# The gate blocks of layer 1, taken in pairs by seven block products over halves of features and tokens

## The chip, the cores and the metric

The kernel runs on one core of a Trainium2 chip. The metric is the device time of one execution in microseconds (us), here the median of several executions on the chip. The instructions of a core are spread over engines with a queue each: TensorE (PE, matrix products; its weight loads are shown as PEld), VectorE (DVE), ScalarE (ACT), GpSimd (POOL) and SyncE (SP, which issues most of the transfers). Each engine works through its own queue in order; engines wait for one another by semaphores.

## What is computed

The reference is one step of a two-layer encoder over 512 prompt and 64 sample tokens. The change lies in layer 1, whose input projection gives four things: the query latent `cq`, the key and value latent `ckv`, the rotary key `kr` and a `gate` of 2048 features.

```python
def odd_layer(x, past, w_in, q_norm_w, kv_norm_w, w_uq, w_ukv, w_out, ln_g, ln_b):
    cq, ckv, kr, gate = split_cols(x @ w_in, SPLIT1)      # 512, 512, 64, 2048 columns
    cq = rms_norm(cq, q_norm_w)
    ckv = rms_norm(ckv, kv_norm_w)
    q = (cq @ w_uq).reshape(b, t, C_HEADS, QK_NOPE + QK_ROPE)
    q_rope = rope(q[..., QK_NOPE:], q_pos)
    kr = rope(kr, q_pos)
    ...
    kv = (lat @ w_ukv).reshape(b, p_len + t, C_HEADS, QK_NOPE + V_DIM)
    ...
    o = o.reshape(b, t, C_WIDTH) * jax.nn.silu(gate)
    y = layer_norm(ALPHA * x + o @ w_out, ln_g, ln_b)
    return y, (ckv, kr)
```

All of it is fp32.

## The kernel before

The activations lie transposed in SBUF: 2048 features as 16 tiles of 128, by T = 576 tokens (512 prompt, 64 sample), in two halves of HALF = 288. TensorE has no fp32 product of full width, so each number is kept as a high part that TensorE takes (`xh`, `whi`) and a remainder (`xl`, `wlo`), and each product is three matmuls: high by high, high by remainder, remainder by high (`mm3`, L175 to L179). A matmul here takes a weight block of 128x128 and 288 tokens.

Weights come from memory in units of 128x1024, which is eight 128x128 blocks: SP loads the unit into a `wraw` tile (L96, two buffers), ScalarE rounds it into `whi` (L110), VectorE takes the remainder into `wlo` (L111). `whi` and `wlo` have four buffers each, so the ScalarE rounding of a unit waits until TensorE is done with the unit four places back. An output block of 128 features (`dense_block`, L153) takes two units, 16 feature tiles and two token halves: 96 matmuls into the two banks of one PSUM tile `pd` (`psd`, two buffers), and then a function (`post`) evacuates the tile.

Layer 1 begins with `quad` (L1085), which forms the four `cq` blocks beside the last layer norm of layer 0. Then, in this order: four blocks of `ckv` (L1244 ff., the last of them starts `c_norm`, which normalises the latent, splits it into `ar[8]` to `ar[15]` and stores it), one block for `kr` with its rotation (`post_kr`, `finish_kr`), and 16 gate blocks. `post_gate` (L1254 to L1258) takes a finished gate block through `silu_from` (L637 to L639: a scaled copy, a tanh and one VectorE operation) and SP stores it in `gts`. Then come the rotary queries in eight `half_unit` pieces (L1275 ff.), each with a copy out of PSUM (L1291), a swap of halves by transfers and a rotation on POOL and DVE (L1237 to L1239), and then the attention, head by head, which multiplies its output by the gate (L1344). Background work (`spawn`, `tick`) is woven in by generators, and a scheduler of the framework orders the instructions of each engine. Waits go by tile: whoever writes a tile waits for the last one that read any part of it.

## Time and profile before

| | |
|---|---|
| median of 3 runs | 2431.32 us (2430.07 to 2433.47) |
| the profiled execution | 2431.8 us |
| its span in the trace | 2430.0 us, so 1.8 us lie around it |
| PE busy | 2387.2 us, 98% of the span |
| DVE, ACT, POOL busy | 1213.7, 825.1, 438.9 us |

Busy times are sums over an engine's instructions. In the trace, consecutive matmuls overlap: one takes some 0.3 us from its start to its end, while the next starts 0.13 us after it. So the time of a run of matmuls is read from the spacing of their starts, and a wait of TensorE shows as a gap between starts. A window view gives, for a stretch of the execution, how long each engine was busy in it and at what share of its full clock TensorE was granted (PEclk). A row of a group of instructions says how long the engine had sat idle just before them, and what ended that. The lines of the profile are those of the kernel before.

### The profile page before, as it was taken

Reading aid. Unit: us, or ns where it says so; the run is one execution under the profiler, and the core shown is the slowest. Engines: PE = TensorE matmul, PEld = TensorE weight load, DVE = VectorE, ACT = ScalarE, POOL = GpSimd, SP = SyncE. Lnnn points to the kernel's source line nnn. Section 1 sums busy time; section 2 is a strip of 40 time slices with the busy share of each in tenths; the row PEclk is TensorE's granted clock in tenths of the full one; section 3 lists DMA queues with packets and bytes.
Section 4 is the critical chain, followed back from the end, with each engine's and each line's share of the span. In section 5 each row is a group of like instructions: output and inputs, shape, how many; then the busy total and the mean of one; then the engine's idle time right before and its main releaser. Section 6 shows DMA issues by size and latency. Waiting matters only on the chain. (4 is left out here: it accounts for less than half of the span.)

```text
span 2430.0 us, 43034 instructions
## 1 busy us (share of the span) xinstructions
PE 2387.2 (98%) x17978; PEld 2358.6 (97%) x17978; DVE 1213.7 (50%) x2290; ACT 825.1 (34%) x1462; POOL 438.9 (18%) x429
## 2 busy tenths in 40 slices
PE   9999999999999999999999999899999999999997
PEld 8999999999999999999999999899999999999996
DVE  6579784664845433434532223824224665654236
ACT  5442232332323333333431212332222454443233
POOL 0001161523515100000011223400001000001323
PEclk9999999999999999999999999999999999999998
DMA  6322242333323322322543332423334321122232
GB/s 211 113 81 79 92 139 83 124 106 104 133 76 128 110 100 91 100 91 91 170 146 97 103 102 81 152 80 127 103 108 136 121 69 60 63 72 79 103 121 79
DMA packets 96642, 256.69 MB, mean 106 GB/s; under 512 B 11520, under 2 KB 20768, under 8 KB 96448
## 3 DMA queue, kind: packets, MB, share of 16 engines
q1 hardware_dynamic: 94816, 251.44, 30.9%
q8 instruction: 141, 2.31, 0.4%
q10 hardware_dynamic: 1632, 2.51, 0.4%
q14 instruction: 53, 0.43, 0.1%
HBM read 216.37 MB, written 34.87 MB: 103 GB/s over the span
## 5 line engine op out<-in xcount | busy, mean ns | idle before, releaser
L179 PE MATMUL pd<-xh,whi 128*128 128x288 f32 x4128 | 894.7, 298 | 6.4 <-ACT whi L135 4.9
L179 PE MATMUL pd<-xh,wlo 128*128 128x288 f32 x4128 | 890.6, 296 | 0.0
L179 PE MATMUL pd<-xl,whi 128*128 128x288 f32 x4128 | 888.3, 296 | 0.0
L111 DVE TENSOR_TENSOR wlo<-wraw,whi 128x1024 fp32r<-128x1024 f32 x307 | 383.1, 1249 | 693.5 <-ACT whi L110 690.4
L179 PEld LDWEIGHTS pd<-xh,whi 128*128 128x128 f32 x4128 | 664.8, 188 | 12.3 <-ACT whi L135 5.2
L179 PEld LDWEIGHTS pd<-xh,wlo 128*128 128x128 f32 x4128 | 665.3, 188 | 1.0
L179 PEld LDWEIGHTS pd<-xl,whi 128*128 128x128 f32 x4128 | 664.5, 188 | 1.2 <-DVE xl L1347 0.2
L110 ACT CAST whi<-wraw 128x1024 fp32r<-128x1024 f32 x308 | 322.3, 1048 | 949.6 <-PE pd L179 922.0
L179 PE MATMUL pd<-ar,whi 128*128 128x288 f32 (+1 forms) x1120 | 211.1, 306 | 6.3 <-DVE xl L1367 4.3
L998 POOL TENSOR_TENSOR f<-f 128x576 f32<-128x576 f32 (+1 forms) x26 | 60.0, 2306 | 687.0 <-DVE f L991 687.0
L179 PEld LDWEIGHTS pd<-ar,whi 128*128 128x128 f32 x1120 | 170.3, 190 | 7.6 <-issue 3.9
L179 PE MATMUL pd<-ar,wlo 128*128 128x288 f32 (+1 forms) x560 | 125.6, 304 | 0.0
L179 PEld LDWEIGHTS pd<-ar,wlo 128*128 128x128 f32 x560 | 92.6, 189 | 0.0
L991 DVE SCALAR_TENSOR_TENSOR f<-f,pd 128x576 f32<-128x576 f32 (+3 forms) x35 | 23.3, 667 | 119.1 <-PE pd L179 91.2
L1406 PE MATMUL pd<-whi,ar 128*128 128x256 f32 (+1 forms) x384 | 74.1, 285 | 0.0
L625 DVE SCALAR_TENSOR_TENSOR f<-f,cw 128x579 f32<-128x579 f32 x72 | 61.4, 853 | 1.2
L1237 POOL TENSOR_TENSOR f<-f 128x576 f32<-128x576 f32 (+1 forms) x9 | 17.5, 1948 | 235.8 <-DMA f<-f 231.6
L1406 PEld LDWEIGHTS pd<-whi,ar 128*128 128x128 f32 (+1 forms) x384 | 57.9, 180 | 0.4
L1406 PE MATMUL pd<-wlo,ar 128*128 128x256 f32 (+1 forms) x192 | 54.3, 283 | 0.0
L739 DVE TENSOR_SCALAR G<-R,ncn 128x128 f32<-128x128 f32 (+1 forms) x160 | 46.9, 363 | 13.2 <-PE pt L758 6.9
L353 ACT ACTIVATE s<-ps,nmc 128x128 f32<-128x128 f32 (+4 forms) x80 | 40.7, 509 | 33.1 <-DVE nmc L1337 32.6
L331 ACT COPY pt<-pt 128x128 f32<-128x128 f32 (+1 forms) x64 | 27.4, 428 | 69.8 <-PE pt L330 64.1
(335 smaller groups left out, 2865.6 us busy)
## 6 DMA issues: line engine op xcount, KB each, us to landing
wraw<-in_wall SPq DMA_DIRECT2D x316, 512.0 KB, 3.5
f<-in_xT SPq DMA_DIRECT2D x32, 288.0 KB, 4.6
R<-rows SPq DMA_DIRECT2D x32, 288.0 KB, 3.3
mixs<-f SPq DMA_DIRECT2D x24, 288.0 KB, 3.2
f<-mixs SPq DMA_DIRECT2D x24, 288.0 KB, 5.9
ea<-rows SPq DMA_DIRECT2D x32, 144.0 KB, 3.2
ys<-f SPq DMA_DIRECT2D x16, 288.0 KB, 2.3
gts<-f SPq DMA_DIRECT2D x16, 288.0 KB, 3.9
```

The lines of the kernel that those rows point to most:

```text
L110: A.copy(hi[:, c], r)
L111: eng.tensor_sub(lo[:, c], r, hi[:, c].bitcast(F32))
L179: PE.matmul(out(hf), a, b(hf), start=start and s == 0, stop=stop and s == 2)
L331: A.copy(pt[:, 0:(j + 1) * 128], p[:, 0:(j + 1) * 128])
L353: A.activation(s[:rows_, :n], (s if src is None else src)[:rows_, :n], AF.Exp, bias=nm[:rows_], scale=scale, accum_out=sums[:rows_, 0:1])
L625: V.scalar_tensor_tensor(a, raw[:, j:j + 579], w(j), a, op0=OP.mult, op1=OP.add)
L739: V.tensor_scalar(G[:m, cs], R[:m, cs], ncn[:m, i, h:h + 1], 0.0, op0=OP.add, op1=OP.min)
L991: V.scalar_tensor_tensor(v(y[:, c]), v(x[:, c]), ALPHA, ev(ps) if n == T else ps, op0=OP.mult, op1=OP.add)
L998: eng.tensor_add(S12[0][:, c], S12[0][:, c], y[:, c])
L1237: PL.tensor_mul(sw[:n, :T], sw[:n, :T], ropet[1][:n, :T])
L1406: PE.matmul(ps[:m, hf, :256], a[k][:, c0:c0 + m], b[:, w], start=(k == 0 and s == 0), stop=(k == 3 and s == 2))
```

## The change

The 16 gate blocks are taken as eight pairs. A pair is a 2x2 block matrix of weights (two output blocks by two halves of the 2048 features: `a11`, `a12`, `a21`, `a22`, one unit each) times a 2x2 block matrix of activations (two halves of the features by two halves of the tokens). The usual way takes eight block products of 24 matmuls each; the change forms the same outputs from seven, with sums of weight blocks and sums of activation blocks (the scheme of Strassen in Winograd's form).

- `sums_x` forms the sums of activations once: POOL adds high part and remainder of the 16 tiles back together (L1284, L1285 of the changed kernel), DVE forms four sums of 288 tokens for each of eight k, and ACT and DVE split three of them into high part and remainder (`T2`, `T3`, `T4`). `place_t1` writes the fourth over the right token half of `xh[0..7]`, `xl[0..7]`. These run as background work beside three `cq` blocks.
- `gates` runs the products: for each, 24 matmuls into one bank. A pair has two PSUM tiles of two banks, p1 (a and b) and p2 (c and d), and the products 0 to 6 go to the banks a, d, a, b, c, d, c. Where the list names a bank again, one product is added onto the other there, or the bank is written anew after a copy. Sums of weight units: two POOL additions (L1328, L1329) and two DVE additions (L1334, L1338) of 128x1024 per pair.
- After products 0 and 2 ACT copies bank a (L1382, L1384); after products 2 to 6 DVE adds or subtracts a bank of 128x288 (L1385, L1387, L1389, L1391, L1393). Then tanh and one VectorE operation per output block as before, without the factor one half, which the attention applies (`scalar_tensor_tensor` in place of `tensor_mul`).
- To make room, the order of the projection is changed: `quad` now forms `ckv`, whose normalised latent goes to a DRAM tensor `lats`; then `kr`, then four `cq` blocks, whose raw outputs go to `qraw` and are read back by `c_norm("q")` during the gates. The pool of scratch tiles `f` is released and set up again with 10 buffers, 20 before. `lat_split` reads `lats` back and splits it after the gates, beside the rotary queries.
- `wraw` has five buffers, two before.

```diff
         if u >= n_units or ("raw", u) in wts:
             return
         off, n = units[u]
-        raw = wp.tile([128, 1024], F32, name="wraw", tag="wraw", bufs=2)
+        raw = wraw()
         SP.dma_start(raw[:, :n], dram_ap(io["wall"], off, [[n, 128], [1, n]]))
         wts["raw", u] = raw
+
+    def wraw():
+        return wp.tile([128, 1024], F32, name="wraw", tag="wraw", bufs=5)
+
...
+    def w_pieces(raw):
+        hi = wp.tile([128, 1024], F32R, name="whi", tag="whi")
+        lo = wp.tile([128, 1024], F32R, name="wlo", tag="wlo")
+        A.copy(hi, raw)
+        V.tensor_sub(lo, raw, hi.bitcast(F32))
+        return hi, lo
...
...
+    def post_q(j):
         def post(ps):
             t = f()
             A.copy(two(t[:, :T]), ev(ps))
-            CQ[kind, j] = t
-            if j == 3:
...
     def c_norm(kind):
-        ts_ = [CQ.pop((kind, j)) for j in range(4)]
+        def raw(j):
+            if kind == "kv":
+                return CQ[j]
+            t = f()
+            SP.dma_start(t[:, :T], qraw[j])
+            return t
+
         s = f()
-        A.activation(s[:, :T], ts_[0][:, :T], AF.Square)
+        A.activation(s[:, :T], raw(0)[:, :T], AF.Square)
         for j in range(1, 4):
             q = f()
-            A.activation(q[:, :T], ts_[j][:, :T], AF.Square)
+            A.activation(q[:, :T], raw(j)[:, :T], AF.Square)
...
         for j in range(4):
-            t = ts_[j]
+            t = raw(j)
             c = (G_QN if kind == "q" else G_KVN) + j
             V.scalar_tensor_tensor(t[:, :T], t[:, :T], cg[:, c:c + 1], rb[:, :T], op0=OP.mult, op1=OP.mult)
             if kind == "q":
-                h, l = ar[j], ar[4 + j]
-                A.copy(h[:, :T], t[:, :T])
-                V.tensor_sub(l[:, :T], t[:, :T], h[:, :T].bitcast(F32))
...
...
             else:
                 SP.dma_start(fo["lat"][j], t[:, :T])
-                h, l = ar[8 + j], ar[12 + j]
-                p = f()
-                SP.dma_start(p[:, 0:128], io["latp"][j])
-                for d0, d1, src in ((0, 512, t[:, 0:512]), (640, 704, t[:, 512:576]), (512, 640, p[:, 0:128])):
-                    A.copy(h[:, d0:d1], src)
-                    V.tensor_sub(l[:, d0:d1], src, h[:, d0:d1].bitcast(F32))
+                SP.dma_start(lats[j], t[:, :T])
             yield
...
...
-    spawn(c_norm("q"))
-    for j in range(4):
-        if j == 3:
-            rope_load()
-        dense_block(mvx, 16, post_c("kv", j))
...
...
+    def sums_x(gt):
+
+        for k in range(8):
+            a, b = f(), f()
+            PL.tensor_add(a[:, :T], xh[k].bitcast(F32), xl[k].bitcast(F32))
+            PL.tensor_add(b[:, :T], xh[k + 8].bitcast(F32), xl[k + 8].bitcast(F32))
+            yield
+            if k % 2 == 0:
+                T1.append(f())
+            t1 = T1[k // 2][:, HALF * (k % 2):HALF * (k % 2) + HALF]
+            V.tensor_sub(t1, a[:, L_], a[:, R_])
+            V.tensor_sub(a[:, R_], a[:, R_], b[:, R_])
+            V.scalar_tensor_tensor(b[:, R_], t1, -1.0, b[:, R_], op0=OP.mult, op1=OP.subtract)
+            V.tensor_add(b[:, L_], b[:, L_], b[:, R_])
+            for n_, src in ((3, a[:, R_]), (2, b[:, R_]), (4, b[:, L_])):
+                h, l = (gt.tile([128, HALF], F32R, name=f"T{n_}{x}{k}") for x in "hl")
+                A.copy(h, src)
+                V.tensor_sub(l, src, h.bitcast(F32))
+                TT[n_, k] = h, l
+            yield
+
+    def place_t1(k):
+        t1 = T1[k // 2][:, HALF * (k % 2):HALF * (k % 2) + HALF]
+        A.copy(xh[k][:, R_], t1)
+        V.tensor_sub(xl[k][:, R_], t1, xh[k][:, R_].bitcast(F32))
+
+    X7 = [lambda k: (xh[k][:, L_], xl[k][:, L_]), lambda k: TT[3, k], lambda k: TT[2, k],
+          lambda k: (xh[k + 8][:, L_], xl[k + 8][:, L_]), lambda k: (xh[k][:, R_], xl[k][:, R_]),
+          lambda k: TT[4, k], lambda k: (xh[k + 8][:, R_], xl[k + 8][:, R_])]
+
+    def gates(n):
+
+        u0 = ucur[0]
+        W7, S1 = {}, {}
+        raw = lambda i, j: wts["raw", u0 + 4 * i + j]
+
+        def free(i, j):
+            wts["raw", u0 + 4 * i + j] = None
+
+        def weights(m):
+            i, s = divmod(m, 7)
+            if i >= n:
+                w_split(u0 + 4 * n + s)
+                return
+            a21, a11, a22, a12 = (raw(i, j) for j in range(4))
+            if s == 0:
+                S1[i] = wraw()
+                W7[m] = w_pieces(a11)
+                PL.tensor_add(S1[i], a21, a22)
+                PL.tensor_add(a21, a21, a11)
+            elif s == 1:
+                W7[m] = w_pieces(a21)
+                free(i, 0)
+            elif s == 2:
+                V.tensor_add(a11, S1[i], a11)
+                W7[m] = w_pieces(a11)
+            elif s == 3:
+                W7[m] = w_pieces(a12)
+                V.tensor_add(a12, a12, a11)
+                free(i, 1)
+            elif s == 4:
+                W7[m] = w_pieces(S1.pop(i))
+            elif s == 5:
+                W7[m] = w_pieces(a22)
+                free(i, 2)
+            else:
+                W7[m] = w_pieces(a12)
+                free(i, 3)
+
+        late = []
+        for m in range(7 * n):
+            i, s = divmod(m, 7)
+            if m == 0:
+                weights(0)
+                weights(1)
+            for at, j in ((0, 0), (2, 1), (4, 2), (5, 3)):
+                if s == at:
+                    w_load(u0 + 4 * (i + 1) + j)
+            weights(m + 2)
+            if s == 0:
+                p1, p2 = psd(), psd()
+                a, b, c, d = (p[:, h, :HALF] for p in (p1, p2) for h in range(2))
+                z0, z1 = f(), f()
+            if i == 0 and s < 2:
+                for k in range(4):
+                    place_t1(4 * s + k)
+                if s == 1:
+                    T1.clear()
+                    spawn(c_norm("q"))
+            if s == 3:
+                for o, z in late:
+                    SP.dma_start(gts[o], z[:, :T])
+                late.clear()
+            hi, lo = W7.pop(m)
+            bank = (a, d, a, b, c, d, c)[s]
+            for k in range(8):
+                w = slice(128 * k, 128 * k + 128)
+                h, l = X7[s](k)
+                for j, (m_, x) in enumerate(((hi[:, w], h), (hi[:, w], l), (lo[:, w], h))):
+                    PE.matmul(bank, m_, x, start=s in (0, 1, 3, 4) and k + j == 0, stop=k == 7 and j == 2,
+                              skip_group_check=True)
+            if s == 0:
+                A.copy(z0[:, L_], a)
+            elif s == 2:
+                A.copy(z0[:, R_], a)
+                V.tensor_sub(z1[:, R_], d, z0[:, R_])
+            elif s == 3:
+                V.tensor_add(z0[:, L_], z0[:, L_], b)
+            elif s == 4:
+                V.tensor_sub(z1[:, R_], z1[:, R_], c)
+            elif s == 5:
+                V.tensor_sub(z1[:, L_], d, z0[:, R_])
+            elif s == 6:
+                V.tensor_add(z0[:, R_], z0[:, R_], c)
+            if s in (5, 6):
+
+                o, z = ((2 * i + 1, z1), (2 * i, z0))[s - 5]
+                th = f()
+                A.activation(th[:, :T], z[:, :T], AF.Tanh, scale=0.5)
+                V.scalar_tensor_tensor(z[:, :T], th[:, :T], 1.0, z[:, :T], op0=OP.add, op1=OP.mult)
+                late.append((o, z))
+            tick()
+        for o, z in late:
+            SP.dma_start(gts[o], z[:, :T])
+        ucur[0] += 4 * n
+
+    spawn(c_norm("kv"))
+    rope_load()
     dense_block(mvx, 16, post_kr, m=64)
-    for j in range(16):
-        dense_block(mvx, 16, post_gate(j))
-    cqh, cql, lah, lal = ar[0:4], ar[4:8], ar[8:12], ar[12:16]
+    dense_block(mvx, 16, post_q(0))
+    drain()
+    ropet.clear()
+    fpool[0].release()
+    fpool[0] = tc.alloc_tile_pool(name="fs", bufs=10, reuse_waits="tile")
+    gt = tc.alloc_tile_pool(name="gt", bufs=1, side="right", reuse_waits="tile")
+    spawn(sums_x(gt))
+    whole.update(range(ucur[0] + 6, ucur[0] + 6 + 32))
+    for j in range(1, 4):
+        dense_block(mvx, 16, post_q(j))
+    while len(TT) < 24:
+        tick()
+    gates(8)
+    gt.release()
+    rope_load()
+    rl = tc.alloc_tile_pool(name="rl", bufs=1, side="right", reuse_waits="tile")
+    lah, lal = ([rl.tile([128, 704], F32R, name=f"la{x}{j}") for j in range(4)] for x in "hl")
+
+    def lat_split():
+        for j in range(4):
+            t, p = f(), f()
+            SP.dma_start(t[:, :T], lats[j])
+            SP.dma_start(p[:, 0:128], io["latp"][j])
+            yield
+            h, l = lah[j], lal[j]
+            for d0, d1, src in ((0, 512, t[:, 0:512]), (640, 704, t[:, 512:576]), (512, 640, p[:, 0:128])):
+                A.copy(h[:, d0:d1], src)
+                V.tensor_sub(l[:, d0:d1], src, h[:, d0:d1].bitcast(F32))
+
+    spawn(lat_split())
 
...
-            V.tensor_mul(g[:, c], o, g[:, c])
+            V.scalar_tensor_tensor(g[:, c], o, 0.5, g[:, c], op0=OP.mult, op1=OP.mult)
             if j == 4:
...
-    four = [_units_of(_blk(w_in1, r(128 * o))) for o in range(4)]
+    four = [_units_of(_blk(w_in1, r(128 * o))) for o in range(4, 8)]
     units.extend(four[o][a] for a in range(2) for o in range(4))
-    for o in range(4, 8):
+    units.extend(_units_of(_blk(w_in1, r(1024, 64))))
+    for o in range(4):
         units.extend(_units_of(_blk(w_in1, r(128 * o))))
-    units.extend(_units_of(_blk(w_in1, r(1024, 64))))
-    for o in range(16):
-        units.extend(_units_of(_blk(w_in1, r(1088 + 128 * o))))
+    for o in range(0, 16, 2):
+        (a11, a12), (a21, a22) = (_units_of(_blk(w_in1, r(1088 + 128 * (o + e)))) for e in range(2))
+        units.extend((a21, a11, a22, a12))
     half = lambda w, cols: w[:, cols].reshape(4, 128, -1).transpose(1, 0, 2).reshape(128, -1)
...
```

**TensorE where one product follows another, second pair.** Before, the next block goes to another tile. In the changed kernel the third product of a pair (T2, bank a) and the fourth (xh8, bank b) go to one tile `pd_17741`, and the sixth (T4, bank d) and seventh (xh8, bank c) to `pd_17742`.

```order
L1379 MATMUL pd_17741<-T2h7_17414,whi_17737 128x288
L1379 MATMUL pd_17741<-T2l7_17415,whi_17737 128x288
L1379 MATMUL pd_17741<-T2h7_17414,wlo_17738 128x288
L1379 MATMUL pd_17741<-xh8_96,whi_17775 128x288
L1379 MATMUL pd_17741<-xl8_112,whi_17775 128x288
L1379 MATMUL pd_17741<-xh8_96,wlo_17776 128x288
```

The first matmul on `xh8` waits for the copy L1384 of the other bank of that tile; it stands directly behind the last matmul on `T2`.

**ScalarE in the same pair.** Before, the roundings of the weights (L110) and the evacuations of a finished block (L637, L638) alternate:

```order
L110 CAST whi_19126<-wraw_19015 128x1024
L637 ACTIVATE f_19041<-pd_18932 128x576
L638 ACTIVATE f_19042<-f_19041 128x576
L110 CAST whi_19187<-wraw_19076 128x1024
L110 CAST whi_19261<-wraw_19130 128x1024
L637 ACTIVATE f_19156<-pd_19047 128x576
```

Now the copy of bank a that the fourth product waits for stands behind the rounding of the seventh product's weights, `whi_17874`, which takes the buffer of `whi_17737`, the weights of the third product:

```order
L110 CAST whi_17841<-wraw_17615 128x1024
...
L110 CAST whi_17874<-wraw_17655 128x1024
L1384 COPY f_17743<-pd_17741 128x288
L110 CAST whi_17906<-wraw_17809 128x1024
L110 CAST whi_17940<-wraw_17734 128x1024
```

So the copy starts only after that rounding, and the rounding only when the third product is nearly through.

**VectorE at the end of the sums over the activations.** The rows are from the remainder of the weights of the fourth product (`wlo_17478`) to the last remainder that the third product of the first pair takes (`T2l7`). Apart from the two `wlo` all of them are new; before, VectorE had one operation of `silu_from` for every second `wlo`.

```order
L111 TENSOR_TENSOR wlo_17478<-wraw_17332,whi_17477 128x1024
L1290 TENSOR_TENSOR f_17385<-f_17381 128x288
L1338 TENSOR_TENSOR wraw_17332<-wraw_17332,wraw_17187 128x1024
L1291 TENSOR_TENSOR f_17381<-f_17381,f_17382 128x288
L1304 TENSOR_TENSOR xl6_110<-f_17385,xh6_94 128x288
L111 TENSOR_TENSOR wlo_17536<-wraw_17422,whi_17535 128x1024
L1292 SCALAR_TENSOR_TENSOR f_17382<-f_17385,f_17382 128x288
...
L1297 TENSOR_TENSOR T3l7_17411<-f_17402,T3h7_17410 128x288
L1293 TENSOR_TENSOR f_17403<-f_17403 128x288
L1297 TENSOR_TENSOR T2l7_17415<-f_17403,T2h7_17414 128x288
```

The sums of the last two k stand behind the fourth product's `wlo`, whose `whi` takes the buffer of the last unit of the `cq` blocks.

## Rows read from the trace of the kernel before

**Rows 1.** The page: span and busy time of each engine.

```profile
span 2430.0 us, 43034 instructions
...
PE 2387.2 (98%) x17978; PEld 2358.6 (97%) x17978; DVE 1213.7 (50%) x2290; ACT 825.1 (34%) x1462; POOL 438.9 (18%) x429
```

**Rows 2.** Windows by engine, from the blocks of ckv through the gates; columns first.

```profile
core 0: us, PE busy (x) PEld busy (x) DVE busy (x) ACT busy (x) POOL busy (x), PEclk, DMA share, GB/s
1600.00:1667.00 67.00, 67.00 (x510) 67.00 (x509) 30.34 (x52) 23.61 (x38) 6.30 (x4) 1.00 0.34 112
1667.00:1858.40 191.40, 191.40 (x1438) 191.40 (x1437) 48.21 (x46) 49.99 (x60) 0.00 (x0) 1.00 0.33 107
```

**Rows 3.** The tile gts: the 16 stores, shortest/median/longest issue, first and last start.

```profile
L1257 SPq DMA_DIRECT2D gts<-f x16: 326/327/327, 1667.1 to 1858.4; - x16
```

**Rows 4.** Lines in the gate stage, 1667 to 1858: busy, mean ns, idle before.

```profile
L111 DVE TENSOR_TENSOR wlo<-wraw,whi 128x1024 fp32r<-128x1024 f32 x30 | 36.8, 1226 | 142.4 <-ACT whi L110 142.4
L110 ACT CAST whi<-wraw 128x1024 fp32r<-128x1024 f32 x30 | 31.4, 1047 | 141.4 <-PE pd L179 141.4
L639 DVE SCALAR_TENSOR_TENSOR f<-f 128x576 f32<-128x576 f32 x16 | 12.1, 758 | 0.8
L638 ACT ACTIVATE f<-f 128x576 f32<-128x576 f32 x15 | 10.3, 687 | 0.6
```

**Rows 5.** Timeline about 1500: start, duration; PSUM's last matmul and the reader behind it.

```profile
1499.62 0.29 PE L1034 MATMUL pd<-ar,wlo 128*128 128x288 f32 x1
...
1500.01 0.46 DVE L991 SCALAR_TENSOR_TENSOR f<-f,pd 128x288 f32<-128x288 f32 x1 [7.48 <-PE pd L1034]
```

**Rows 6.** Lines from 1500 to 1582 (the stage of quad).

```profile
L1103 ACT COPY f<-pd 128x288 f32<-128x288 f32 x6 | 2.0, 402 | 4.5 <-PE pd L1098 4.5
...
L998 DVE TENSOR_TENSOR f<-f 128x288 f32<-128x288 f32 x1 | 0.5, 459 | 0.1
```

**Rows 7.** Timeline about 1890: VectorE's result, and TensorE that waited for it.

```profile
1889.60 0.75 DVE L1367 TENSOR_TENSOR xl<-pd,xh 128x576 fp32r<-128x576 f32 x1
...
1890.41 0.91 PE L179 MATMUL pd<-ar,whi 128*128 128x352 f32 x4 [0.66 <-DVE xl L1367]
```

**Rows 8.** TensorE's waits for copies out of pd by ScalarE: total us, times, longest us.

```profile
PE pd L1098 <- ACT f L1103: 2.0, 1, 2.0
PE pd L179 <- ACT f L1291: 2.0, 2, 1.7
```

**Rows 9.** Timeline about 1396: additions of POOL, beside VectorE and alone.

```profile
1396.29 1.23 DVE L111 TENSOR_TENSOR wlo<-wraw,whi 128x1024 fp32r<-128x1024 f32 x1
1396.38 2.42 POOL L998 TENSOR_TENSOR f<-f 128x576 f32<-128x576 f32 x1 [15.02 <-DVE f L991]
...
1398.76 1.43 POOL L999 TENSOR_TENSOR f<-f 128x576 f32<-128x576 f32 x1
```

**Rows 10.** Timeline about 1864: VectorE's L111 begun while POOL works.

```profile
1863.55 1.92 POOL L1237 TENSOR_TENSOR f<-f 128x576 f32<-128x576 f32 x1 [202.87 <-DMA f<-f]
...
1864.10 2.45 DVE L111 TENSOR_TENSOR wlo<-wraw,whi 128x1024 fp32r<-128x1024 f32 x1
```

**Rows 11.** Windows by engine in the stage of quad; columns as in rows 2.

```profile
1530.00:1540.00 10.00, 8.55 (x64) 8.12 (x63) 9.77 (x27) 4.48 (x9) 5.12 (x6) 1.00 0.11 36
1540.00:1552.00 12.00, 10.55 (x72) 9.64 (x73) 12.00 (x13) 3.62 (x7) 12.00 (x13) 1.00 0.31 112
1552.00:1565.00 13.00, 10.96 (x71) 10.73 (x70) 11.88 (x27) 6.98 (x16) 0.75 (x1) 0.87 0.70 269
```

**Rows 12.** Windows by engine in the stage of the rotary queries; columns as in rows 2.

```profile
1865.00:1877.50 12.50, 12.19 (x92) 11.96 (x92) 9.60 (x8) 3.08 (x5) 6.07 (x4) 1.00 0.58 173
1877.50:1890.00 12.50, 10.57 (x78) 10.10 (x77) 10.25 (x10) 4.25 (x6) 5.15 (x4) 1.00 0.71 211
1890.00:1902.50 12.50, 8.48 (x39) 8.22 (x40) 6.35 (x7) 2.33 (x3) 2.85 (x2) 0.78 0.54 195
```

**Rows 13.** Lines from 1640 to 1670: VectorE's part of splitting the kv latent.

```profile
L1220 DVE TENSOR_TENSOR ar<-f,ar 128x512 fp32r<-128x512 f32 (+2 forms) x12 | 5.3, 492 | 0.0
```

More of the change, by code (lines that the diff above doesn't have):

```diff
@@ L86, in tile_step @@
     qrs = dp.tile([8, 128, T], F32, name="qrs")
+    qraw = dp.tile([4, 128, T], F32, name="qraw")
+    lats = dp.tile([4, 128, T], F32, name="lats")
     wts = {}
@@ L94, in w_load @@
         off, n = units[u]
-        raw = wp.tile([128, 1024], F32, name="wraw", tag="wraw", bufs=2)
+        raw = wraw()
         SP.dma_start(raw[:, :n], dram_ap(io["wall"], off, [[n, 128], [1, n]]))
         wts["raw", u] = raw
+    def wraw():
+        return wp.tile([128, 1024], F32, name="wraw", tag="wraw", bufs=5)
+    whole = set()
+    def w_pieces(raw):
[4 more added lines that the diff above has]
+        return hi, lo
     def w_split(u, eng=V):
@@ L102, in w_split @@
         w_load(u)
+        if u in whole:
+            return
         n = units[u][1]
@@ L126, in w_part @@
         if ("raw", u) not in wts:
-            wts["raw", u] = wp.tile([128, 1024], F32, name="wraw", tag="wraw", bufs=2)
+            wts["raw", u] = wraw()
             wts["hi", u] = wp.tile([128, 1024], F32R, name="whi", tag="whi")
@@ L1172, in tile_step @@
         quad(32, 36)
-    CQ = {("q", j): cq[j] for j in range(4)}
+    CQ = list(cq)
+    cq.clear()
     S12.clear()
@@ L1176, in tile_step @@
     LNR.clear()
-    arp.pop().release()
-    def post_c(kind, j):
+    while arp:
+        arp.pop().release()
+    ra = tc.alloc_tile_pool(name="ra", bufs=1, side="right", reuse_waits="tile")
+    cqh, cql = ([ra.tile([128, T], F32R, name=f"cq{x}{j}") for j in range(4)] for x in "hl")
+    def post_q(j):
         def post(ps):
@@ L1183, in post @@
             A.copy(two(t[:, :T]), ev(ps))
-            CQ[kind, j] = t
-            if j == 3:
-                spawn(c_norm(kind))
+            SP.dma_start(qraw[j], t[:, :T])
         return post
     def c_norm(kind):
-        ts_ = [CQ.pop((kind, j)) for j in range(4)]
+        def raw(j):
[4 more added lines that the diff above has]
+            return t
         s = f()
-        A.activation(s[:, :T], ts_[0][:, :T], AF.Square)
+        A.activation(s[:, :T], raw(0)[:, :T], AF.Square)
         for j in range(1, 4):
             q = f()
-            A.activation(q[:, :T], ts_[j][:, :T], AF.Square)
+            A.activation(q[:, :T], raw(j)[:, :T], AF.Square)
             PL.tensor_add(s[:, :T], s[:, :T], q[:, :T])
+        del q
         yield
@@ L1209, in c_norm @@
             if kind == "q":
-                h, l = ar[j], ar[4 + j]
-                A.copy(h[:, :T], t[:, :T])
-                V.tensor_sub(l[:, :T], t[:, :T], h[:, :T].bitcast(F32))
+                A.copy(cqh[j], t[:, :T])
+                V.tensor_sub(cql[j], t[:, :T], cqh[j].bitcast(F32))
             else:
                 SP.dma_start(fo["lat"][j], t[:, :T])
-                h, l = ar[8 + j], ar[12 + j]
-                p = f()
-                SP.dma_start(p[:, 0:128], io["latp"][j])
-                for d0, d1, src in ((0, 512, t[:, 0:512]), (640, 704, t[:, 512:576]), (512, 640, p[:, 0:128])):
-                    A.copy(h[:, d0:d1], src)
-                    V.tensor_sub(l[:, d0:d1], src, h[:, d0:d1].bitcast(F32))
+                SP.dma_start(lats[j], t[:, :T])
             yield
+        if kind == "kv":
+            CQ.clear()
     def swap_halves(dst, src, n):
@@ L1252, in finish_kr @@
         yield
-    def post_gate(j):
-        def post(ps):
-            g = silu_from(ps)
-            SP.dma_start(gts[j], g[:, :T])
-        return post
-    spawn(c_norm("q"))
-    for j in range(4):
-        if j == 3:
-            rope_load()
-        dense_block(mvx, 16, post_c("kv", j))
-    dense_block(mvx, 16, post_kr, m=64)
-    for j in range(16):
-        dense_block(mvx, 16, post_gate(j))
-    cqh, cql, lah, lal = ar[0:4], ar[4:8], ar[8:12], ar[12:16]
+    L_, R_ = slice(0, HALF), slice(HALF, T)
@@ new lines, in tile_step @@
+    TT = {}
+    T1 = []
+    def sums_x(gt):
[17 more added lines that the diff above has]
+            yield
@@ new lines, in place_t1 @@
+    def place_t1(k):
[15 more added lines that the diff above has]
+                w_split(u0 + 4 * n + s)
+                return
+            a21, a11, a22, a12 = (raw(i, j) for j in range(4))
[77 more added lines that the diff above has]
+        ucur[0] += 4 * n
@@ L1427, in tile_step @@
     o_src[0] = ys
-    arp[0].release()
+    rl.release()
+    ra.release()
     tp = tc.alloc_tile_pool(name="tp", bufs=1, side="right", reuse_waits="tile")
@@ L1684 @@
     arrays, table = _layout({k: np.asarray(v) for k, v in inputs.items()})
-    nc = _bacc.Bacc("TRN2", target_bir_lowering=False, num_devices=1)
+    nc = _bacc.Bacc("TRN2", target_bir_lowering=False, num_devices=1, dynamic_dma_scratch_size=1024)
     io = {k: nc.dram_tensor(f"in_{k}", v.shape, _mybir.dt.from_np(v.dtype), kind="ExternalInput").ap()
```

## The prediction

> **What bounds the kernel now.** The page first: TensorE is busy 2387.2 of 2430.0 us [rows 1], so the kernel is a stream of matmuls, and a change pays if it shortens the stream without putting gaps in. The windows confirm it for the stage that is changed: from 1600 to 1858 us TensorE is busy all the time at a granted clock of 1.00, while VectorE and ScalarE are busy about a quarter of the gate stage and POOL not at all [rows 2]. In the lines of that stage the idle time of ScalarE's rounding ends with TensorE, and that of VectorE's remainder with ScalarE [rows 4]: both run after TensorE and never ahead of it. The price of a matmul comes from the stores of the gates: 16 stores, 15 blocks from 1667.1 to 1858.4 us [rows 3], so 12.75 us for a block, 0.133 us for each of its 96 matmuls.
>
> **The matmuls that go.** A pair took two blocks, 25.51 us. The program has 168 matmuls of the same size for it, 22.32 us at the same spacing. That is 3.19 us less, and 25.5 us for eight pairs: the whole of what the change can gain.
>
> **The waits that come.** Waits go by tile, and a tile holds two banks. Within a pair the program makes TensorE wait for an evacuation at three places where one product follows another directly. I build each from durations: the reader starts 0.39 us after the last matmul's start [rows 5], an operation of 288 tokens takes 0.40 on ScalarE and 0.46 on VectorE [rows 5, 6], and TensorE goes on 0.06 after the result (1889.60 + 0.75 to 1890.41 [rows 7]); 0.13 of it is the ordinary spacing.
> - Product 3 (bank b) waits for the copy of bank a (L1384). On ScalarE that copy stands behind the rounding of product 6's weights, 1.05 us [rows 4], which waits for the last but one matmul of product 2: 0.39 - 0.13 + 1.05 + 0.40 + 0.06 - 0.13 = 1.64 us.
> - Product 6 (bank c) waits for L1391, the read of bank d after product 5: 0.39 + 0.46 + 0.06 - 0.13 = 0.78 us.
> - Product 1 of the next pair (bank d) waits for L1393, the read of bank c after product 6: 0.78 us. Behind L1391, VectorE first has a `wlo`, the gate's last operation and L1338, 1.23 + 0.76 us [rows 4] and 1.23 for L1338, as wide as a `wlo`, which just fits beside product 6 (3.19 us).
>
> The other evacuations (L1382, L1385, L1387, L1389) have a whole product between them and the next writer, 3.19 us, and I cost them at nothing; if that cover went, each would cost 0.8. Together 3.20 us a pair: what the seven products save, the waits take back, 0.0 net.
>
> **POOL in the pairs.** Two POOL additions of 128x1024 a pair run beside VectorE. When VectorE began a remainder 0.55 us into a POOL operation of 1.92, it took 2.45 us instead of 1.23 [rows 10]: 1.2 us later. Remainders are prepared two products ahead, so most of that is hidden; between 0 and 1.2 us a pair, I take 0.25, near the hidden end, as only product 0's remainder stands there. Eight pairs: +2 us.
>
> **The start of the gates.** Count from the end of `quad`. One `kr` and four `cq` blocks take 5 x 12.75 = 63.8 us, product 0 ends at 67.0. TensorE then takes T3 and T2 with k = 6 and 7 last, and needs the last remainder of T2 (`T2l7`) at 72.9 us to go on without a stop. VectorE cannot have it: `wlo_17478` stands ahead of it and belongs to a `whi` whose buffer is free when the last `cq` unit is through, at 63.8. With 0.39 + 1.05 + 0.06 it starts at 65.3; it, L1338 and another `wlo` take 3.7, 15 operations of 288 tokens 0.46 each [rows 6], 6.9: 75.9 us. So at least a 3 us stop. The other bound takes VectorE as loaded. From 33.3 us (the `wlo` of the fifth block's first unit, by the same buffer rule) it has seven `wlo` and two additions, 11.1 us, and 60 operations of 288, 27.6 us; that makes 72.0 without POOL. POOL has 12 additions of 576 and two of 1024 still to do. What of a POOL addition shuts VectorE out? In 12 us of `quad`, 13 operations of each of 288 tokens filled both engines [rows 11]: 0.92 us for one of each, of which VectorE's is 0.46 to 0.51, so at least 0.41 is POOL's, 0.83 for 576. Beside the remainder it was 1.22 [rows 10]. So 13.0 to 19.0 us with the wide ones in proportion, and `T2l7` at 85 to 91, unless it falls into time in which VectorE waits anyway. I take the middle of 75.9 and 85.0, 80.5, since VectorE waits often for ScalarE's halves of the same chain: a stop of 8 us, ends 3 and 18.
>
> On this the Trainium skill, "SBUF — State Buffer" (Terms), has a harder rule: VectorE and GpSimd share a port pair by an exclusive lock held for the full instruction, and the loser blocks entirely. The trace agrees where a remainder met POOL [rows 10] and where POOL met a remainder (2.42 us, 1.43 alone [rows 9]), less in `quad` [rows 11]; by the rule the additions would cost 1.43 us each and proportionally more for the wide ones, 22 us, and the sum would be 2457.
>
> **The rotary queries.** `lat_split` moves from a stage in which TensorE never waited to one where it does. There VectorE is busy 26.2 of 37.5 us and TensorE only 31.2 [rows 12]. The split costs VectorE 5.3 us [rows 13], its loads start behind the last gate store on SP, and half of the scratch buffers remain. Between 0 (it fills VectorE's idle time) and 7 (all on the path, with a little for the clock, 0.78 there); I take 3, about half.
>
> **At nothing.** The attention's multiplication has the same tile and engine. The added transfers (32 of 288 KB at most) are covered by transfer engines that are a third busy [rows 2]; the earlier weight loads may move some stage by 1 or 2 us either way. The latent's and rotary key's own work runs beside TensorE's blocks as before.
>
> **Sum.** The profiled execution is 2431.8 us, 0.5 above the median of the runs. 2431.8 + 0 (matmuls less waits) + 2 + 8 + 3 = 2444.8, on the median 2444.3, rounded to **2444**. A measurement of this kernel can tell about 0.2%, 4.9 us, from no change.
>
> **The rivals.**
> - *The waits are short* (faster). TensorE's wait is only the evacuation itself, because the reader's start overlaps the last matmul's drain and the rounding ahead of the copy is done early: 0.5 us at each of the three places, 1.5 a pair. For it: six copies by L1103 out of `pd` [rows 6] cost TensorE one wait [rows 8]. Against: the order of ScalarE, and the 2.0 that the one wait was. With a stop of 3 and no cost at the rotary queries: 2431.8 - 25.5 + 12 + 2 + 3 = 2423.3, on the median 2423. It decides for faster when the waits are below 1.95 us a pair (25.5 - 5 - 4.9 = 15.6, by eight).
> - *Everything near the lower bound* (no change). Waits as forecast, stop 3, nothing at the rotary queries: 2436.8, on the median 2436. VectorE's idle share in the stage before speaks for it.
> - *POOL shuts VectorE out for nearly its whole operation.* Stop of 18: 2454.8, on the median 2454. The remainder of 2.45 us speaks for it [rows 10], `quad` against [rows 11].
> - *The clock falls in the gates.* In `quad`, a stretch of 13 us with 2 us of gaps had a granted clock of 0.87 [rows 11], and the last stretch of the rotary queries 0.78 [rows 12]. At 0.87 the 178 us of products would take 27 us more: 2471. Against: the stretches from 1530 to 1552, with 1.45 us idle in 10 and in 12, stayed at 1.00 [rows 11], and the pairs would be idle 3.2 of 25.5. The Trainium skill, "TensorE: Matmul & The Clock Gate" (A second HAM failure mode: psum-queue depth-cycling), speaks for this rival: a kernel that cycled through PSUM banks idled briefly between groups, often enough for its clock to swing. By it the sum would be about this rival's; `quad` bears it out in one stretch of three [rows 11].
>
> **How the numbers follow.** Chances: forecast 0.38, POOL 0.15, clock 0.07, so slower 0.6; no change 0.2; short waits, faster, 0.2. The range, 2422 to 2455, takes in the no-change case, the upper half of the short-wait case and the POOL case but not the clock's: about 0.8. For the forecast alone it would be 2437 to 2451.
>
> **What would show it.** Right: a wait of TensorE for L1384 some eight times at 1.6 us, for L1391 and L1393 at 0.8; pairs of gate stores 25 to 26 us apart; one stop of about 8 us for a `T2l` or `T3l` early in the first pair; VectorE and POOL both full just before; gaps a little longer in the rotary queries. Wrong: pairs at 24 us or less (the waits are short), a stop under 3 or over 18 us, a granted clock below 1.00 in the pairs, or a gap in a stage that the change does not touch.

## The result, and the profile after

The changed kernel takes 2458.23 us (median of 4 runs, 2455.22 to 2459.70), the kernel before 2432.28 us beside it: a ratio of 1.0106, 95% interval 1.0089 to 1.0124. So it is slower, by 26 us, where 2444 and a range up to 2455 were forecast. The profiled execution took 2455.22 us, its span is 2453.4 us, 23.4 us longer than before [rows 1]. It is the fastest of the four: traces here account for these 23.4 us, not for the 3 us by which the median lies above it.

The page's first part shows that the change does what it says: 192 matmuls fewer, and yet a lower share of busy time.

```profile
span 2453.4 us, 43059 instructions
...
PE 2376.8 (97%) x17786; PEld 2339.1 (95%) x17786; DVE 1332.1 (54%) x2434; ACT 857.5 (35%) x1518; POOL 519.4 (21%) x461
```

TensorE's waits, longest in total first (us in total, times, longest). None of those on L1379, the matmuls of the pairs, existed before; L1461 is the old L1291 [rows 8]. Lines are those of the changed kernel.

```profile
PE pd L1379 <- ACT f L1384: 11.2, 8, 1.6
PE pd L196 <- ACT f L1461: 8.4, 5, 3.8
...
PE pd L1379 <- DVE f L1393: 4.5, 7, 0.7
...
PE pd L1379 <- DVE f L1391: 4.4, 8, 0.6
PE pd L1379 <- ACT f L1203: 4.3, 1, 4.3
```

The three waits of the pairs are there as often as forecast: 1.4, 0.64 and 0.55 us each, counted from the recorded end of the matmul before. L1203, the evacuation of the last `cq` block, was in no term of the sum.

**The pairs.** TensorE's timeline, the places where a pair waits, and the first product (T3) of the next pair:

```profile
1713.29 0.40 PE L1379 MATMUL pd<-xh,whi 128*128 128x288 f32 x1 [0.55 <-DVE f L1391]
1717.38 0.37 PE L1379 MATMUL pd<-T3h,whi 128*128 128x288 f32 x1 [0.64 <-DVE f L1393]
1725.33 0.40 PE L1379 MATMUL pd<-xh,whi 128*128 128x288 f32 x1 [1.36 <-ACT f L1384]
...
1743.35 0.37 PE L1379 MATMUL pd<-T3h,whi 128*128 128x288 f32 x1 [0.64 <-DVE f L1393]
```

From the second pair on, T3 begins every 25.93 us (1691.81 to 1847.41 over six pairs); two blocks took 25.51 before [rows 3]. The seven products alone would be 22.32. So 3.6 us a pair go. From start to start, less the ordinary 0.13, the three waits cost 1.52, 0.71 and 0.80 us; the matmul behind each comes 0.21 to 0.24 us later, not 0.13, which is another 0.3 a pair; and 0.4 go where product 0 waits for its `wlo`.

**The first pair.** The same stretch in windows of 5 us (PE, PEld, DVE, ACT, POOL busy, granted clock, transfers):

```profile
1645.00:1650.00 5.00, 3.49 (x27) 3.26 (x25) 5.00 (x13) 3.04 (x7) 5.00 (x1) 1.00 0.17 68
1650.00:1655.00 5.00, 2.20 (x9) 2.20 (x10) 4.87 (x6) 2.13 (x4) 5.00 (x3) 0.59 0.28 86
1655.00:1660.00 5.00, 4.05 (x22) 3.71 (x21) 5.00 (x6) 2.24 (x5) 2.95 (x2) 0.72 0.08 32
1660.00:1665.00 5.00, 2.53 (x15) 1.78 (x13) 4.23 (x11) 2.71 (x7) 0.23 (x1) 0.96 0.93 316
1665.00:1670.00 5.00, 2.96 (x8) 2.03 (x9) 4.87 (x6) 4.00 (x7) 2.58 (x2) 0.50 0.22 72
1670.00:1675.00 5.00, 5.00 (x23) 5.00 (x23) 1.48 (x2) 0.09 (x1) 4.69 (x3) 0.52 0.30 105
```

TensorE is idle for 9.8 us of the first five windows, while VectorE is full. The granted clock falls in the first stop (0.59 and 0.72), comes back, and is at half, 1.2 GHz, for ten more us from 1665. The first product T3 begins 4.3 us late, and the second pair's 39.0 us behind it instead of 25.9: 17.4 us are lost.

The starts of the matmuls divide them. Some 12 us go until the last operands of T3 are there, at 1666.5, about 2 of them in matmuls that run at half clock. Behind that 25 more matmuls at half clock, 0.24 us apart or more instead of 0.13, cost 3.2 us, and 2.1 us are matmuls of the latent's norm, which now stand in this pair.

Why VectorE was late shows in the timeline of the sums. First, at 1610, it and POOL alternate: an operation that takes VectorE 0.45 us alone is recorded with 1.5 to 1.7, because each waits for the other to end.

```profile
1609.65 1.68 DVE L1290 TENSOR_TENSOR f<-f 128x288 f32<-128x288 f32 x1
...
1610.97 1.64 POOL L1285 TENSOR_TENSOR f<-xh,xl 128x576 f32<-128x576 f32 x1
1611.43 1.50 DVE L1291 TENSOR_TENSOR f<-f 128x288 f32<-128x288 f32 x1
1612.57 1.65 POOL L1284 TENSOR_TENSOR f<-xh,xl 128x576 f32<-128x576 f32 x1
1612.96 1.58 DVE L1292 SCALAR_TENSOR_TENSOR f<-f 128x288 f32<-128x288 f32 x1
```

Then one addition of POOL takes 11.6 us, while VectorE begins 22 operations, most of them 0.37 us apart. And on ScalarE the evacuation L1203 has the casts of the sums before it:

```profile
1640.84 11.60 POOL L1284 TENSOR_TENSOR f<-xh,xl 128x576 f32<-128x576 f32 x1 [3.01 <-DVE T4l L1297]
...
1650.84 0.43 ACT L1296 CAST T4h<-f 128x288 fp32r<-128x288 f32 x1 [0.62 <-DVE f L1293]
1651.18 1.04 ACT L110 CAST whi<-wraw 128x1024 fp32r<-128x1024 f32 x1
...
1652.12 0.63 ACT L1203 COPY f<-pd 128x576 f32<-128x576 f32 x1
...
1652.80 0.61 PE L1379 MATMUL pd<-T3h,whi 128*128 128x288 f32 x1 [4.32 <-ACT f L1203]
...
1662.31 0.44 DVE L1291 TENSOR_TENSOR f<-f 128x288 f32<-128x288 f32 x1
...
1663.95 0.68 ACT L1219 ACTIVATE f<-f 128x576 f32<-128x576 f32 x1 [1.11 <-DMA f<-qraw]
1664.54 0.41 ACT L1296 CAST T3h<-f 128x288 fp32r<-128x288 f32 x1
1665.01 0.61 PE L1379 MATMUL pd<-T3h,whi 128*128 128x288 f32 x1 [1.30 <-ACT T3h L1296]
...
1666.78 0.45 DVE L1297 TENSOR_TENSOR T2l<-f,T2h 128x288 fp32r<-128x288 f32 x1
```

The addition that waited is that of k = 6, and the operands of k = 7 come last, `T2l` at 1667.2. The cast of `T3h` of k = 7 had its sum at 1662.8 (L1291), but stood behind a square of `c_norm("q")` (L1219) that waited for its block to be read back: some 1.7 us later. Neither the long addition nor the place of L1203 decides when the sums end. In e12 below, with the same sums, the same addition took 2.34 us, L1203 came only at 1657.0, and the last `T2l` 0.2 us later than here:

```profile
1640.84 2.34 POOL L1284 TENSOR_TENSOR f<-xh,xl 128x576 f32<-128x576 f32 x1 [3.00 <-DVE T4l L1297]
...
1657.02 0.63 ACT L1203 COPY f<-pd 128x576 f32<-128x576 f32 x1
...
1667.00 0.44 DVE L1297 TENSOR_TENSOR T2l<-f,T2h 128x288 fp32r<-128x288 f32 x1
```

**The rotary queries.** ScalarE waits for a load of `lat_split` (the casts L1435) with the evacuation L1461 behind it, and TensorE waits for that:

```profile
1878.52 0.97 ACT L1435 CAST lah<-f 128x512 fp32r<-128x512 f32 x3 [4.05 <-DMA f<-in_latp]
...
1881.94 0.76 ACT L1435 CAST lah<-f 128x512 fp32r<-128x512 f32 x2 [1.51 <-DMA f<-lats]
1882.61 0.63 ACT L1461 COPY f<-pd 128x576 f32<-128x576 f32 x1
...
1883.30 0.85 PE L196 MATMUL pd<-cqh,whi 128*128 128x288 f32 x2 [3.77 <-ACT f L1461]
```

**The account** of the 23.4 us, by the starts of the same things in both traces: `quad` ends 3.1 us earlier (1579.1, 1582.2); from there to the first gate matmul (1645.2, 1649.4) 1.1 us less, since the second latent's statistics now fall into the gates; the gates, without 24 matmuls of the rotary queries that stand among them now, 223.9 us for 205.9, 18.0 more (17.4 in the first pair and 0.42 in each of seven, less 1.3 because the last pair has none behind it to wait, and 1.0 for matmuls of the norm that stood there before too); from their end to the attention's first product with the values (1942.5, 1920.8), the 24 matmuls counted here, 73.4 us for 65.5, 8.0 more; from there to the end 1.7 more.

### The profile page after: what moved, and what is told of

Its sections match the earlier page's. It is cut to its first block, busy times and chain, and to the rows that moved or that the text cites. A ratio compares the mean times of both kernels' runs of the same rounds, so it can differ in the third digit from the quotient of the medians.

```text
span 2453.4 us, 43059 instructions
## 1 busy us (share of the span) xinstructions
PE 2376.8 (97%) x17786; PEld 2339.1 (95%) x17786; DVE 1332.1 (54%) x2434; ACT 857.5 (35%) x1518; POOL 519.4 (21%) x461
## 5 line engine op out<-in xcount | busy, mean ns | idle before, releaser
L196 PE MATMUL pd<-xh,whi 128*128 128x288 f32 (+1 forms) x3616 | 786.0, 298 | 6.5 <-ACT whi L152 5.0
L196 PE MATMUL pd<-xh,wlo 128*128 128x288 f32 (+1 forms) x3616 | 778.9, 296 | 0.0
L196 PE MATMUL pd<-xl,whi 128*128 128x288 f32 (+1 forms) x3616 | 778.7, 296 | 0.0
L196 PEld LDWEIGHTS pd<-xh,whi 128*128 128x128 f32 (+1 forms) x3616 | 582.3, 188 | 12.4 <-ACT whi L152 5.3
L196 PEld LDWEIGHTS pd<-xh,wlo 128*128 128x128 f32 (+1 forms) x3616 | 582.3, 188 | 0.9
L196 PEld LDWEIGHTS pd<-xl,whi 128*128 128x128 f32 (+1 forms) x3616 | 581.2, 188 | 1.1 <-DVE xl L1517 0.2
L111 DVE TENSOR_TENSOR wlo<-wraw,whi 128x1024 fp32r<-128x1024 f32 x56 | 76.7, 1370 | 43.6 <-ACT whi L110 43.6
L110 ACT CAST whi<-wraw 128x1024 fp32r<-128x1024 f32 x56 | 58.6, 1048 | 118.0 <-PE pd L1379 77.0
L1379 PE MATMUL pd<-xh,whi 128*128 128x288 f32 x256 | 78.2, 305 | 15.6 <-ACT f L1384 11.2
L1379 PE MATMUL pd<-xh,wlo 128*128 128x288 f32 x256 | 77.0, 301 | 0.6
L1379 PE MATMUL pd<-xl,whi 128*128 128x288 f32 x256 | 76.4, 299 | 0.0
L1379 PEld LDWEIGHTS pd<-xh,whi 128*128 128x128 f32 x256 | 49.1, 192 | 19.4 <-ACT f L1384 13.2
```

The costliest lines, as they stand in the source:

```text
L110: A.copy(hi, raw)
L111: V.tensor_sub(lo, raw, hi.bitcast(F32))
L196: PE.matmul(out(hf), a, b(hf), start=start and s == 0, stop=stop and s == 2)
L1379: PE.matmul(bank, m_, x, start=s in (0, 1, 3, 4) and k + j == 0, stop=k == 7 and j == 2, skip_group_check=True)
```

## The experiments

Theory A, from the trace: three separate losses, the stop in the first pair with the clock behind it, the waits in the pairs, `lat_split`. All compare with the changed kernel's 2458.23 us; ratios are to the kernel before, run beside them.

**e1, without the sums.**

```diff
-    spawn(sums_x(gt))
...
-                for k in range(4):
-                    place_t1(4 * s + k)
...
-          lambda k: TT[4, k], lambda k: (xh[k + 8][:, R_], xl[k + 8][:, R_])]
+          lambda k: (xh[k + 8][:, R_], xl[k + 8][:, R_]), lambda k: (xh[k + 8][:, R_], xl[k + 8][:, R_])]
```

> Leaves out the sums of the activations (sums_x, place_t1): the seven products take plain halves of xh and xl instead, so the output is another one; matmuls, weight sums, evacuations and waits in the pairs stay. Theory A (the start of the gates is lost to VectorE and POOL being late with the sums, 9.8 us of idle TensorE, and to the clock that falls after it, 8.5 us): the stop in the first pair goes, the time falls by 13 to 18 us against the changed kernel, to about 2442, and the granted clock stays at 1.00 in the first pair. Rival (the first pair stops because c_norm for q reads its blocks back at that time): falls by at most 4 us, stop and low clock stay.

Measured in a single execution: 2442.47 us, 15.8 below the changed kernel's median and 12.8 below its profiled execution; by the trace the gates take 212.1 us instead of 223.9. The granted clock is 1.00 in every window of 5 us from 1645 to 1680, and beyond the waits of every pair TensorE waits only 2.5 us for a `whi` and 0.4 for a `wlo`. So the sums cost most of what the first pair loses, and the read-back of q, which is still there, does not stop it by itself. It is not free: the `whi` waited for POOL's sum of weights, which ran beside VectorE's split of q, and a stretch at half clock followed (0.84 and 0.82 in the windows from 1690 to 1700).

**e2, other banks together.**

```diff
-                a, b, c, d = (p[:, h, :HALF] for p in (p1, p2) for h in range(2))
+                a, d, b, c = (p[:, h, :HALF] for p in (p1, p2) for h in range(2))
```

> Banks a and d share a PSUM tile, and b and c (before a with b, c with d); the scheduler then puts product 3 between 0 and 1, and no product follows directly on an evacuation that it waits for. Theory A (the pairs lose what they save to the three waits, 2.55 us, and about 0.7 us of restarting after them): spacing of pairs 22.5 to 23.2 us instead of 25.9, no wait for L1384, L1391 or L1393, the time 20 to 26 us below the changed kernel, about 2434. Rival (products of 24 matmuls are slower in themselves, or VectorE and ScalarE set the pace of a pair): spacing stays over 24.5, the time falls by less than 12 us.

Measured: 2428.93 us, ratio 0.9992 (0.9983 to 1.0001): level with the kernel before. One line takes 29 us off by the medians, 25.5 between the two profiled executions, where 20 to 26 were expected. In the windows of two whole pairs TensorE does not stop, and T3 begins every 22.34 us, the 168 matmuls at the old spacing:

```profile
1718.50:1740.80 22.30, 22.30 (x170) 22.25 (x169) 14.57 (x16) 9.23 (x11) 5.66 (x2) 1.00 0.35 127
1740.80:1763.20 22.40, 22.40 (x171) 22.33 (x170) 14.59 (x16) 9.22 (x11) 5.68 (x2) 1.00 0.38 123
```

So nothing but the waits by tile, with their restarts, held the pairs. The wait on POOL's additions went with them: their work is the same. What stayed, in this execution in one piece, is the stop at the start:

```profile
PE pd L1379 <- ACT f L1203: 9.4, 1, 9.4
PE pd L196 <- ACT f L1461: 8.6, 4, 5.0
```

**e3, the sums set off a block earlier.**

```diff
     dense_block(mvx, 16, post_kr, m=64)
-    dense_block(mvx, 16, post_q(0))
     drain()
...
-    for j in range(1, 4):
+    for j in range(4):
```

> The scratch pool is set up again and sums_x started before the first cq block instead of behind it: 12.75 us more for the same work. Theory A: the stop in the first pair is mostly gone with its low clock, 10 to 16 us below the changed kernel, about 2445. Rival (the read-back of q, or the evacuation order on ScalarE, sets the stop): within 4 us of the changed kernel.

Measured: 2461.16 us, ratio 1.0126 (1.0109 to 1.0143): no gain. The trace says why it is no test of the time available: POOL's first addition starts at 1605.2 us, in the changed kernel at 1604.2. The sums had been waiting for POOL's rotation of `kr` and for VectorE's part of the latent's norm, not for their place in the program. TensorE waited 12.9 us for L1203, which made that evacuation the next thing to look at.

**e4, the casts of `lat_split` later.**

```diff
             SP.dma_start(p[:, 0:128], io["latp"][j])
             yield
+            yield
+            yield
```

> lat_split waits three ticks instead of one between the loads of a block and its casts, so that ScalarE does not stand waiting for a transfer ahead of the evacuations of the rotary queries (L1461). Theory A (that order costs the stage of the rotary queries its 6 us): waits of TensorE for L1461 fall from 8.4 to under 4 us, the time by 3 to 6 us, to about 2454. Rival (VectorE's 5 us more of work, or half the scratch buffers, cost it): within 2 us of the changed kernel.

Measured: 2454.44 us, ratio 1.0098 (1.0083 to 1.0113): 3.8 less, but the intervals overlap, and between the profiled executions it is 0.3. The waits for the evacuation (now L1463) stay at 8.3 us in total, the longest is 2.0 instead of 3.8, and from the last gate matmul on `xh` to the attention it is 68.1 us instead of 70.7. At most a part of the cause.

**e6, matmuls that fill the first stop.**

```diff
+            if i == 0 and s == 0:
+                dm = pss()
+                for r_ in range(4):
+                    for k in range(8):
+                        w = slice(128 * k, 128 * k + 128)
+                        PE.matmul(dm[:, :HALF], hi[:, w], xh[k + 8][:, L_], start=k == 0, stop=k == 7, skip_group_check=True)
```

> 32 matmuls of 128x288 more, behind product 0 of the first pair, into a PSUM tile that nobody reads: they fill the first 4.3 us in which TensorE stands still there, and do nothing else. Theory A (8.5 us of the first pair's loss is the clock that falls because TensorE stands still): the granted clock stays at 1.00 until 1653 us, less of the pair runs at half speed, and the time falls by 3 to 8 us, to about 2452. Rival (the loss is the late operands alone, the low clock only runs beside the waiting): the time is the same or up to 4 us longer.

Measured: 2463.11 us, ratio 1.0133 (1.0119 to 1.0147): 4.9 us longer, though the intervals overlap. The clock held where the filling was, and fell in the next stop:

```profile
1650.00:1655.00 5.00, 4.77 (x36) 4.54 (x36) 4.87 (x8) 2.35 (x4) 5.00 (x3) 1.00 0.11 43
1655.00:1660.00 5.00, 1.29 (x10) 1.05 (x8) 5.00 (x4) 0.73 (x2) 3.81 (x2) 0.91 0.25 75
1660.00:1665.00 5.00, 3.10 (x10) 2.43 (x11) 5.00 (x14) 4.25 (x9) 0.00 (x0) 0.50 0.74 245
```

TensorE then waited 4.49 us for T3 of k = 6, at 1660.78. POOL's addition took 11.63 us here as well. The time did not fall, against theory A: the operands of k = 6 and 7 set the end, and what T3's first matmuls gained at full clock was waited away. What the clock costs afterwards this run does not separate; by the starts of the matmuls it is 3.2 us in the changed kernel, not the 8.5 of theory A. The low clock came later with the later stop (0.56 from 1665 to 1670), the matmuls on T2, part of which had run between the last k of T3, now all ran behind T3 of k = 6, most of them at half clock, and the second pair took 30.5 us, with a stop of 3.7 us for the copy L1384 (here L1390).

**e8, loads in place of POOL's additions.** What `ys` holds lacks the layer norm's bias; e8 and e9 leave that out.

```diff
-            PL.tensor_add(a[:, :T], xh[k].bitcast(F32), xl[k].bitcast(F32))
-            PL.tensor_add(b[:, :T], xh[k + 8].bitcast(F32), xl[k + 8].bitcast(F32))
+            SP.dma_start(a[:, :T], ys[k])
+            SP.dma_start(b[:, :T], ys[k + 8])
```

> POOL's 16 additions of high part and remainder (L1284, L1285) are replaced by loads of the same blocks from the DRAM tensor ys, which holds them in fp32. Theory B (the stop is the evacuation of the last cq block, L1203, which stands on ScalarE behind casts of the sums that wait for VectorE, and VectorE is late because each POOL addition shuts it out for about 1.2 us): VectorE's operations of 288 tokens take 0.45 us throughout, L1203 comes in time, the stop falls under 3 us and the time by 11 to 16 us, to about 2445. Rival (the number of operations on VectorE and the order on ScalarE are enough to make them late): falls by less than 5 us.

Measured: 2446.77 us, ratio 1.0061 (1.0046 to 1.0076): 11.5 less, theory B. VectorE's operations now start every 0.37 us, L1203 comes at 1649.0 instead of 1652.1, and TensorE no longer waits for it; what is left of the stop, beside a wait of 2.7 us for L1384, are waits of 1.1 us or less:

```profile
PE pd L1379 <- ACT whi L110: 1.1, 1, 1.1
PE pd L1379 <- DVE T2l L1297: 0.5, 2, 0.3
...
PE pd L1379 <- ACT T3h L1296: 0.5, 1, 0.5
```

A stretch at half clock stays (0.54 from 1660 to 1665 us), and the first pair still takes 33.6 us. The run takes away two things at once, that POOL shuts VectorE out and that VectorE has to wait for POOL's results; it does not part them.

**e9, e2, e4 and e8 together.**

> e2, e4 and e8 together: banks paired so that no product waits for an evacuation, loads in place of POOL's additions, the casts of lat_split further behind their loads. If the three causes are separate their gains add up: 2458 - 29 - 13 - 3 = 2413 us, clearly faster than the kernel before. If the first pair's stop only moves (the loads are late, or SP's queue holds up weights), 2422 to 2430.

Measured: 2419.45 us, ratio 0.9951 (0.9938 to 0.9963), 6 us short of the full sum. In the gates the gains add up: 188.6 us, 35.3 less than the changed kernel, where e2 alone has 23.9 and e8 10.0 less. What is missing is e4's: from the gates to the attention it is 74.0 us, 73.4 in the changed kernel and 70.9 in e4, and TensorE waits 10.3 us for the evacuations there.

**e11, the same with the bias.**

```diff
+            A.activation(b[:, :T], b[:, :T], AF.Identity, bias=cg[:, cb:cb + 1])
-            V.tensor_sub(a[:, R_], a[:, R_], b[:, R_])
+            V.scalar_tensor_tensor(a[:, R_], a[:, R_], cg[:, ca:ca + 1], b[:, R_], op0=OP.add, op1=OP.subtract)
```

> As e9, with the layer norm's bias added to the blocks that come from ys, which holds them without it: 8 ScalarE operations of 576 tokens (0.7 us each) while the last cq blocks run, and the other half in a VectorE operation that was there. If ScalarE has room for that, within 3 us of e9, 2417 to 2423 us, faster than the kernel before by 0.3 to 0.6%; if ScalarE's queue holds the last cq block's evacuation up again, 2425 or more.

Measured: 2421.16 us (2420.57 to 2422.94), ratio 0.9965 (0.9951 to 0.9979). This version leaves nothing of the computation out, and is faster than the kernel before, by 9 us. TensorE's longest waits between 1570 and 1950 us show what it still leaves:

```profile
PE pd L196 <- ACT f L1465: 9.2, 4, 5.1
PE pd L1381 <- DVE f L1387: 4.4, 1, 4.4
```

**e12, without `lat_split`.**

> The changed kernel with lat_split left out: its loads, casts and subtractions are replaced by eight memsets on POOL, so the latent is zero and the output another one. Theory A (the 5 us that the stage of the rotary queries lost are lat_split's): 4 to 7 us below the changed kernel, about 2453, with the waits for L1461 and the time from the last gate matmul to the first attention product back near those of the kernel before. Rival (half of the scratch buffers or the late rotation tables cost it): within 2 us of the changed kernel.

Measured: 2451.81 us, ratio 1.0090 (1.0076 to 1.0103), 6.4 less by the medians, whose intervals overlap, and 3.9 between the profiled executions. The trace agrees with the second: the attention's first product with the values comes at 1938.8 instead of 1942.5 with the gates' last matmul on `xh` at 1871.8 in both, so `lat_split` has 3.7 of the 8.0 us. The waits for the evacuation fall to 5.8 us, still more than before [rows 8]. The rest, 4.3 us (the rotation tables loaded anew behind the gates, or fewer scratch buffers) was not tried apart.

## Why the prediction was right or wrong

**Right: the matmuls that go, and the waits that come.** 25.5 us were to be saved, and the waits were to eat them. They did: 3.6 us a pair against 3.2 + 0.25 forecast, so +0.4 net a pair, about 3 us in all, where +2 was forecast. e2 shows it from the other side: without the waits the pairs are 22.34 us. Counted as the forecast counts them, from start to start less 0.13, the waits are 1.52, 0.71 and 0.80 us where 1.64, 0.78 and 0.78 were worked out. The sum did not have the 0.1 us on the matmul behind each. With e2 the 0.4 us on product 0's `wlo` vanished too: it may have stood there because the scheduler had put product 0 ahead of product 5, which was not tried apart.

**Wrong: the start of the gates**, a stop of 8 us forecast, ends 3 and 18; 17.4 were lost. Of the 10.4 us by which the profiled execution passed the sum, this term has 9.4, the largest part. The step that failed is "I take the middle of 75.9 and 85.0": it let half of POOL's work fall into time in which VectorE waits anyway. There was hardly any such time; VectorE is recorded busy 37.6 of the 40 us before 1640, and its operations from 1604 to 1640 with 18 us more than they take alone (0.45, 0.75 and 1.22 us by width). `T2l7` came 88 us behind the end of `quad`, 86 without the 2.3 us that TensorE's own stream took longer than the 63.8 forecast. That is the other bound, "`T2l7` at 85 to 91", and makes a stop of 12 to 13 us; some 12 were measured. The rest was in no term: 3.2 us of half clock behind the stop, and the norm's 2.1. Product 1 was taken to need its operands alone, while its PSUM tile is the last `cq` block's, whose evacuation waits on ScalarE behind the sums' casts; that wait only says where the stop falls, as e12 shows. The clock was a rival for all pairs; it fell in and behind the stop, and stayed at 1.00 in all later pairs of the changed kernel, with their 3 us of waits, so that rival was wrong in place.

That the sums, and in them POOL's additions, make the operands late is shown by e1 and e8. That VectorE and POOL wait for one another is read from the recorded durations. On this the rule was cited from the Trainium skill, "SBUF — State Buffer" (Terms), that the loser of the shared port pair blocks entirely: the trace agrees, in both directions (VectorE 1.50 to 1.68 instead of 0.45, POOL 1.65 instead of 1.43). The sum by that rule, 2457, was the nearest number in the prediction, but in part by luck: it takes a stop of 21 us.

**Wrong in size: the rotary queries**, 3 forecast, 8.0 measured. The prediction priced VectorE's 5.3 us; the wait was on ScalarE, whose casts stood waiting for transfers ahead of the evacuations. e12 gives 3.7 us of it to `lat_split`; the rest is open. Without this miss the median would have been inside the range too.

**At nothing: mostly right.** -3.1, -1.1 and +1.7 us elsewhere. The 1.1 are matmuls of the norm that moved into the first pair. Where the first 3.1 come from was not followed.

**The rivals.** Short waits did not happen with this order, but the version with no waits exists: one line away, e2. "POOL shuts VectorE out for nearly its whole operation", 2454, was the closest of them and had 0.15; its stop of 18 us is 6 more than was measured, and the clock and the rotary queries made up for it.

## What to carry to other kernels

Waits go by tile, so which banks share a tile decides whether a scheme with fewer products gains anything: put banks together that are written and read at different times, and see in the order which product stands directly behind a reader of its tile. Before moving elementwise work beside a full TensorE, ask of each engine's queue what waits there for whom: an evacuation behind casts that wait for another engine or for a transfer can be a stall of TensorE, however little work ScalarE has. VectorE and POOL, where both take two operands from SBUF as here, are nearly one engine in time; a load from memory can take the place of POOL's half.

## What was not expected of the hardware

POOL can starve. An addition of 128x576 that takes 1.4 us alone [rows 9] took 11.60 us in the changed kernel, with VectorE's operations going on one after another, and 11.63 in e6. Before, the trace showed only delays of about one operation [rows 9, 10]. It does not always: e12, with the same sums, had 2.34 in that place, and VectorE waited instead. What lets POOL in is not shown; the last sums came at the same time either way. And after a wait of half a us or more, the matmul that TensorE takes up again is followed by the next after 0.21 to 0.24 us instead of 0.13, at the full granted clock.
